# Layer 0 of a two-layer transformer backbone: background weight loads on GpSimd's queue, and attention A's value products two items later

## The chip, the cores and the metric

One Trainium2 chip, of which this program uses one core. The core has five engines that run their own instruction streams in order: TensorE (PE, matrix products), VectorE (DVE), ScalarE (ACT), GpSimd (POOL) and SyncE (SP, which here only issues DMA transfers). GpSimd can issue DMA transfers as well. The metric is device microseconds (us) for one execution of the whole program; the figure given for a kernel is the median of several runs.

## The reference

A diffusion backbone over 1024 latent tokens and 256 context tokens, width 1024, two layers. Layer 0, where the change lies, runs two attentions side by side and then a mixture of experts:

```
mod = silu(c) @ w_ada[l] + b_ada[l]              # modulation: 6 x 1024 numbers for x, the same for ctx
h   = x * (1 + sc1) + sh1
aq, ak, av, bq, bk, bv = split(h @ ab_w_in)
oa = window_gqa(rope(aq), rope(ak), av, ..., sink)   # A: 8 heads, 2 key heads, window 128 + context
ob = neighbourhood_attn(bq, bk, bv, ..., rpb)        # B: 8 heads, 8 x 16 neighbourhood + context
y  = concat(oa, ob) @ ab_w_out
x  = layer_norm(alpha * x + g1 * y);  then experts, and layer 1 in the same manner
```

Each attention is softmax(scores) times values. The modulation of both layers (`w_ada`, 2 x 1024 x 6144 numbers in float32) doesn't depend on the tokens, so most of it is computed in the background of layer 0's attention.

## The kernel before

Numbers are held as pairs of 16-bit floats (a high part and a rest), so that a product takes three matrix products (`mm3`, L183 to L185), and each probability block is split in two as well.

**Units.** `attn_l0` goes over six units u: two for A (four heads each) and four for B (two heads each). While unit u's attention runs (`attn_unit`), the projection of unit u+1 (`proj_unit`), 16 steps of the background modulation (`ada`, called `bg`) and a bias table are emitted between its steps (`interleave`, a hand-written mix by weights). A scheduler then sets the final order of each engine's instructions from this program order; the order of an engine is fixed before the run, and each engine works through its own in turn.

**One item** of attention is a pair (block t of 128 tokens, head h). It passes through the stages of `pipelined`: `qk` (scores S on PE, L679 to L682), `soft` (row maximum on DVE L702, L703, L705; exponential on ACT L706 for A, L720 and L723 for B; the high part `Ps` on ACT L730), `low` (the rest, on DVE or GpSimd, L737; after the odd head SP issues one DMA transpose for both heads, L739, which writes the transposed probabilities `PT`), two empty stages, and `pv` (value products O on PE from PT; after the last head DVE L771, ACT L774, GpSimd L775 and a store by GpSimd's queue, L776). In step i, `pv` therefore handles item i-5. `Ps` is a ring of two buffers (one per pair of heads), `PT` a ring of three, S has two buffers.

**The background modulation** works in steps n of 512 KB each: a load of `w_ada` (L311) into a ring of three buffers, the high part on ACT (L315), the rest on DVE (L318, which frees the buffer), products on PE (L331). Every fourth step ends a row (L337) that SP stores to DRAM (`mod_d`, L339); the row's start value, `b_ada`, is loaded by GpSimd's queue (L324). 16 of the 96 loads belong to an earlier stage, which passes `tps`; 80 are the background's.

Of the kernel before, what the change touches and what calls it, by code (L numbers as in the profile page):

```python
# [13 lines left out]
F16 = mybir.dt.float16  # L14
# [8 lines left out]
P = 128  # L23
# [50 lines left out]
def pipelined(items, stages):  # L74
    n, depth = len(items), len(stages)
    st = [None] * n
    for i in range(n + depth - 1):
        for s in (0, *range(depth - 1, 0, -1)):
            j = i - s
            if 0 <= j < n:  # L80
                st[j] = stages[s](items[j], st[j])
        yield
# [86 lines left out]
class Kern:  # L169
# [131 lines left out]
    def ada(self, work, pool, pspool, rbufs, hbufs, bbufs, tps=None):  # L301


        nc = self.nc
        raws, parts, rows, sums = {}, {}, {}, {}

        def load(n):
            l, j = work[n // 4]
            cols, k = slice(j * 512, (j + 1) * 512), n % 4 * 2
            raws[n] = pool.tile([P, 2, 512], F32, name="adaraw", bufs=rbufs)  # L310
            nc.sync.dma_start(raws[n], self.i["w_ada"][l].rearrange("(k p) n -> p k n", p=P)[:, k:k + 2, cols])  # L311

        def high(n):
            parts[n] = pool.tile([P, 2, 2, 512], F16, name="adahl", bufs=hbufs)
            nc.scalar.activation(parts[n][:, 0], raws[n], AF.Copy, scale=SW)  # L315

        def low(n):
            nc.vector.scalar_tensor_tensor(parts[n][:, 1], raws[n], SW, parts[n][:, 0], op0=ALU.mult, op1=ALU.subtract)  # L318

        def products(n):  # L320
            if n % 4 == 0:
                l, j = work[n // 4]
                rows[n // 4] = pool.tile([2, 512], F32, name="ada_b", bufs=bbufs)
                (nc.gpsimd if tps is None else nc.sync).dma_start(  # L324
                    rows[n // 4], self.i["b_ada"][l:l + 1, j * 512:(j + 1) * 512].to_broadcast([2, 512]))
                sums[n // 4] = pspool.tile([P, 512], F32, name="ps_ada", tag="proj")
            ps = sums[n // 4]
            for q in range(2):
                k = n % 4 * 2 + q
                for a in range(2):  # L330
                    nc.tensor.matmul(ps, self.sc(k), parts[n][:, a, q],  # L331
                                     start=k + a == 0, stop=k == KD - 1 and a == 1)

        def end(c):
            (l, j), row, ps = work[c], rows[c], sums[c]
            for part in (ps[:2], ps[32:34]):
                nc.vector.scalar_tensor_tensor(row, part, 1.0 / (SA * SW), row, op0=ALU.mult, op1=ALU.add)  # L337
            if j >= 4:
                nc.sync.dma_start(self.mod_d[l, :, j * 512:(j + 1) * 512], row)  # L339
                return  # L340
            pt = (tps or pspool).tile([P, 4, 2], F32, name="ps_adat", tag="O" if tps else "proj")
            for q in range(4):
                nc.tensor.transpose(pt[:, q, :], row[:, q * P:(q + 1) * P], self.id32[:2, :2])
            dst = self.modTs[l][:, j // 2, (j % 2) * 4:(j % 2) * 4 + 4, :]
            if j < 2:
                nc.vector.tensor_scalar_mul(dst, pt, SA)
            else:
                nc.vector.tensor_scalar(dst, pt, 1.0, SA, op0=ALU.add, op1=ALU.mult)

        last = 4 * len(work) - 1  # L350
        for n in range(-1, last + 1):
            for m in range(0 if n < 0 else n + rbufs - 1, min(last, n + rbufs - 1) + 1):
                load(m)
            if n < last:
                high(n + 1)
            if n >= 0:
                low(n)
                products(n)
                if n % 4 == 3:
                    end(n // 4)  # L360
                yield
# [83 lines left out]
def attn_l0(K, moe):  # L445
    nc, tc = K.nc, K.tc
    with ExitStack() as outer:
        big = K.pool("l0big", ctx=outer)
        ctx = outer.enter_context(ExitStack())
# [92 lines left out]
        vring = K.pool("l0v", 2, ctx=ctx)  # L542
        btab = K.pool("l0bt", 2, ctx=ctx)
        pring = K.pool("l0p", 2, ctx=ctx)
        tring = K.pool("l0t", 3, ctx=ctx)
        pctx = ctx.enter_context(ExitStack())
        rp = K.pool("l0rp", ctx=pctx, top=True)

# [83 lines left out]
        def attn_unit(u):  # L632
            isA = u < 2
# [13 lines left out]
            st_t = {}  # L647

            def blocks(t):
                if t >= NX:  # L650
                    return [], [8, 9]
                if isA:
                    return list(range(max(0, t - 1), min(NX, t + 2))), [8, 9]
                a, b = b_key_blocks(t)
                return list(range(a, b)), [8, 9]
# [30 lines left out]
            def soft(it, S):  # L686
                t, h = it
                loc, cx = blocks(t)
                nl, nk = len(loc) * P, (len(loc) + 2) * P
                if not isA and it == inner:  # L690
                    for r, n in ((0, 1), (8, 2)):
                        m = rowm[:, None, r:r + n, None].to_broadcast([P, 2, n, 64])
                        nc.gpsimd.tensor_add(tb[:, :, r + 3:r + 3 + n], tb[:, :, r + 3:r + 3 + n], m)
                if h == 0:
                    st_t[t] = (wk.tile([P, nh], F32, name="nm", tag=f"nm{nh}", bufs=3),
                               wk.tile([P, 2, nh], F32, name="dd", tag=f"dd{nh}", bufs=3))
                nm, dd = st_t[t]
                nmh = nm[:, h:h + 1]
                mx = wk.tile([P, 2], F32, name="mx", bufs=4)
                Pt = pring.tile([P, 896], F32, name="Pt")  # L700
                if isA:
                    nc.vector.reduce_max(mx[:, 0:1], S[:, :nk], axis=AX.X)  # L702
                    nc.vector.tensor_scalar(mx[:, 1:2], mx[:, 0:1], sinkb[:, gh0 + h:gh0 + h + 1], -ESC,  # L703
                                            op0=ALU.max, op1=ALU.mult)
                    nc.vector.tensor_scalar_add(nmh, mx[:, 1:2], LNSP)  # L705
                    nc.scalar.activation(Pt[:, :nk], S[:, :nk], AF.Exp, bias=nmh, scale=ESC,  # L706
                                         accum_out=dd[:, 0, h:h + 1])
                else:
                    nc.vector.reduce_max(mx[:, 0:1], S[:, nl:nk], axis=AX.X)
                    mm = mx[:, 0:1]  # L710
                    if nl:
                        mm = mx[:, 1:2]
                        i0 = loc[0] * 2 - 2 * t + 7
                        bt = tb[:, h, i0:i0 + nl // 64]
                        nc.vector.tensor_tensor_reduce(out=Pt[:, :nl], in0=S[:, :nl],
                                                       in1=bt.rearrange("p a b -> p (a b)"),
                                                       scale=1.0, scalar=mx[:, 0:1], op0=ALU.add, op1=ALU.max,
                                                       accum_out=mm)
                    nc.vector.tensor_scalar(nmh, mm, -ESC, LNSP, op0=ALU.mult, op1=ALU.add)
                    nc.scalar.activation(Pt[:, nl:nk], S[:, nl:nk], AF.Exp, bias=nmh, scale=ESC,  # L720
                                         accum_out=dd[:, 0, h:h + 1])
                    if nl:
                        nc.scalar.activation(Pt[:, :nl], Pt[:, :nl], AF.Exp, bias=nmh, scale=ESC,  # L723
                                             accum_out=dd[:, 1, h:h + 1])
                if h % 2 == 0:
                    st_t[t, "Ps"] = pring.tile([P, 4 * 896], F16, name="Ps")
                    st_t[t, h] = tring.tile([P, 28, P], F16, name="PT")
                Ps, PT = st_t[t, "Ps"], st_t[t, h - h % 2]
                a = (h % 2) * 2 * nk
                nc.scalar.activation(Ps[:, a:a + nk], Pt[:, :nk], AF.Copy)  # L730
                return Pt, Ps, PT, a, nk
# [48 lines left out]
            order = list(range(NT)) if isA else B_ORDER  # L780
            items = [(t, h) for t in order for h in range(nh)]
            inner = (2, 0)
            same = lambda i, s: s
            yield from pipelined(items, [qk, soft, low, same, same, pv])
            done.update(ended)
            if u == 5:
                for area in (qring, vring, btab, pring, tring):
# [1225 lines left out]
@with_exitstack  # L2013
def hybrid_backbone_kernel(ctx: ExitStack, tc: tile.TileContext, ins, out: bass.AP):
    nc = tc.nc
    K = Kern(ctx, tc, ins, out, None)
    K.setup()
    m0, m1 = Moe(K, 0, NT), Moe(K, 1, NX)
    attn_l0(K, m0)
    m0.run()  # L2020
    attn_l1(K, m1)
    final_ln(K, m1, lambda t: out[0, t * P:(t + 1) * P, :])
# [32 lines left out]
```

## Time and profile before

| | |
|---|---|
| Median of 3 runs (lowest, highest) | 3307.09 us (3301.38, 3307.56) |
| The profiled execution: its own time, its span | 3288.79 us, 3286.7 us |
| Busy over the span | PE 79%, DVE 79%, ACT 60%, GpSimd 31% |
| Attention A's units: scores from 105.8 us, last step's DVE work at 366.4 us | the stage 105 to 370 |
| Attention B's units | about 370 to 790 us |

A profile shows one execution: what each engine did and when, what ended its idle time (the releaser), and what the DMA queues moved. An engine's busy share is an average over the stage asked for. The rows below are word for word from such views.

### The profile page before, as it was taken

How to read it: one execution, taken by the hardware profiler on the slowest of the kernel's cores; microseconds unless marked ns; L12 is line 12 of the kernel's file. 1: busy time of each engine (PE TensorE's matmuls, PEld its weight loads, DVE VectorE, ACT ScalarE, POOL GpSimd, SP SyncE). 2: the span in 40 equal slices, each digit the busy share in tenths (PEclk: the TensorE clock that was granted, in tenths of full speed). 3: DMA queues.
4: the chain of work that ended last, by engine and by line, in shares of the span. 5: the costliest groups of instructions: out<-in, count | busy, mean ns of one | idle time of the engine just before them, and what ended most of it. 6: DMA issues, size and time to landing. Idle time of an engine off the chain costs nothing. (4 is left out here: it accounts for less than half of the span.)

```text
span 3286.7 us, 74447 instructions
## 1 busy us (share of the span) xinstructions
PE 2585.5 (79%) x30127; PEld 1790.8 (54%) x30127; DVE 2600.0 (79%) x4496; ACT 1974.0 (60%) x2949; POOL 1018.0 (31%) x652
## 2 busy tenths in 40 slices
PE   6877878868479888987477777877868489998886
PEld 3555545534267777765245554555534367776663
DVE  6787777778897777887767776778877897888986
ACT  5567766754466566776356655556653565666664
POOL 0133333332342222221532322222321473234443
PEclk8999999979789999998679988999978699999998
DMA  7789989789778889998538999645558598999996
GB/s 247 161 179 193 199 202 190 170 208 222 249 264 335 314 328 360 366 377 336 195 102 160 172 159 178 126 99 99 113 125 213 184 345 329 353 376 379 385 373 250
DMA packets 879160, 790.05 MB, mean 240 GB/s; under 512 B 689398, under 2 KB 719366, under 8 KB 878806
## 3 DMA queue, kind: packets, MB, share of 16 engines
q1 hardware_dynamic: 846981, 714.26, 75.4%
q0 software_dynamic: 26336, 69.85, 6.5%
q8 instruction: 239, 3.92, 0.5%
q10 hardware_dynamic: 5488, 1.09, 0.2%
q14 instruction: 116, 0.94, 0.1%
HBM read 565.85 MB, written 64.55 MB: 192 GB/s over the span
## 5 line engine op out<-in xcount | busy, mean ns | idle before, releaser
L375 DVE SCALAR_TENSOR_TENSOR arena<-arena 128x2048 f16<-128x2048 f32 (+4 forms) x439 | 911.1, 2098 | 174.4 <-ACT arena L374 170.3
L374 ACT ACTIVATE arena<-arena 128x2048 f16<-128x2048 f32 (+4 forms) x439 | 748.6, 1725 | 307.5 <-DMA arena<-in_w_gate_up_dram 197.3
L1364 PE MATMUL pg<-arena 128*128 128x72 f16 (+4 forms) x4736 | 635.2, 210 | 93.0 <-DVE arena L1351 70.6
L1366 PE MATMUL pg<-arena 128*128 128x72 f16 (+4 forms) x4736 | 631.9, 210 | 31.1 <-DVE arena L375 22.3
L1365 PE MATMUL pg<-arena 128*128 128x72 f16 (+4 forms) x4736 | 632.5, 210 | 10.0 <-DVE arena L1351 7.5
L183 PEld LDWEIGHTS <-arena 128*128 128x128 f16 (+1 forms) x3488 | 346.7, 103 | 356.0 <-DMA arena<-arena 148.5
L1365 PEld LDWEIGHTS <-arena 128*128 128x128 f16 x4736 | 473.9, 102 | 70.2 <-issue 66.3
L1366 PEld LDWEIGHTS <-arena 128*128 128x128 f16 x4736 | 473.3, 102 | 56.6 <-DVE arena L375 33.3
L1364 PEld LDWEIGHTS <-arena 128*128 128x128 f16 x4736 | 473.9, 102 | 32.9 <-ACT arena L374 18.8
L184 PEld LDWEIGHTS <-arena 128*128 128x128 f16 (+1 forms) x3488 | 346.5, 103 | 194.0 <-issue 99.4
L1381 POOL DMA_INDIRECT y_d<-arena,rt_sidx x74 | 237.9, 3215 | 606.3 <-ACT arena L1394 305.6
L185 PEld LDWEIGHTS <-arena 128*128 128x128 f16 (+1 forms) x3488 | 346.8, 103 | 128.5 <-issue 20.6
L183 PE MATMUL O<-arena 128*128 128x64 f16 (+1 forms) x1744 | 233.5, 210 | 142.7 <-DMA arena<-arena 108.9
L184 PE MATMUL O<-arena 128*128 128x64 f16 (+1 forms) x1744 | 233.0, 210 | 0.0
L185 PE MATMUL O<-arena 128*128 128x64 f16 (+1 forms) x1744 | 232.9, 210 | 0.0
L1774 POOL TENSOR_TENSOR arena<-arena 128x1280 f16<-128x1280 f32 x57 | 151.6, 2659 | 248.6 <-issue 166.0
L1755 ACT ACTIVATE arena<-S,arena 128x1280 f32<-128x1280 f32 x128 | 169.1, 1321 | 92.7 <-DVE arena L1753 81.0
L1344 POOL DMA_INDIRECT arena<-h_d,rt_gidx x74 | 147.3, 1990 | 223.8 <-PE pt L1350 162.4
L1752 DVE TENSOR_REDUCE arena<-S 128x1 f32<-128x1280 f32 x128 | 189.6, 1482 | 26.5 <-PE S L185 17.6
L195 PE MATMUL py<-arena 128*72 128x512 f16 (+4 forms) x592 | 185.9, 395 | 20.7 <-ACT arena L1376 13.9
L197 PE MATMUL py<-arena 128*72 128x512 f16 (+4 forms) x592 | 183.5, 392 | 0.0
L199 PE MATMUL py<-arena 128*72 128x512 f16 (+4 forms) x592 | 180.4, 386 | 0.0
(390 smaller groups left out, 6261.7 us busy)
## 6 DMA issues: line engine op xcount, KB each, us to landing
arena<-in_w_gate_up_dram SPq DMA_DIRECT2D x256, 1024.0 KB
arena<-in_w_down_dram SPq DMA_DIRECT2D x128, 1024.0 KB
arena<-in_w_ada_dram SPq DMA_DIRECT2D x96, 512.0 KB
arena<-y_d SPq DMA_DIRECT2D x36, 512.0 KB
x_d<-arena POOLq DMA_DIRECT2D x18, 512.0 KB, 3.5
h_d<-arena SPq DMA_DIRECT2D x18, 512.0 KB
arena<-x_d SPq DMA_DIRECT2D x18, 512.0 KB
arena<-in_x_dram SPq DMA_DIRECT2D x16, 512.0 KB
```

The source lines that it names most:

```text
L183: mm(ps, lh, rh, start=first, stop=False)
L184: mm(ps, lh, rl, start=False, stop=False)
L185: mm(ps, ll, rh, start=False, stop=last)
L195: mm(ps[:, o], lh, rh[:, o], start=first, stop=False)
L197: mm(ps[:, o], lh, rl[:, o], start=False, stop=False)
L374: nc.scalar.activation(wh, raw, AF.Copy, scale=scale)
L375: nc.vector.scalar_tensor_tensor(wl, raw, scale, wh, op0=ALU.mult, op1=ALU.subtract)
L1364: mm(pg[:, m, :n], wh, xh, start=k == 0 and m % 4 == 0, stop=False)
L1365: mm(pg[:, m, :n], wh, xl, start=False, stop=False)
L1366: mm(pg[:, m, :n], wl, xh, start=False, stop=k == 7 and m % 4 == 3)
L1381: self.K.nc.gpsimd.indirect_dma_start(out=self.K.y_d[self.l], out_offset=bass.IndirectOffsetOnAxis(ap=sidx, axis=0), in_=y[:n], in_offset= ...
L1752: nc.vector.reduce_max(mx[:, 0:1], S[:, :TOK], axis=AX.X)
```

## The change

Three edits, all in layer 0's attention. The background's loads of `w_ada` and the stores of its rows go out on GpSimd's queue and no longer on SP's. In A, two further empty stages stand between `low` and `pv`, so `pv` handles item i-7 in step i; B keeps two. The transposed probabilities get one area of 84 blocks in place of a ring of three tiles of 28 blocks (the same bytes): A cuts it into four slots of 20 blocks, B into three of 28, and the slot follows from the pair's place in its unit, starting at slot 0 in each unit.

```
-            nc.sync.dma_start(raws[n], self.i["w_ada"][l]...)
+            (nc.gpsimd if tps is None else nc.sync).dma_start(raws[n], self.i["w_ada"][l]...)
...
             if j >= 4:
-                nc.sync.dma_start(self.mod_d[l, :, j * 512:(j + 1) * 512], row)
+                nc.gpsimd.dma_start(self.mod_d[l, :, j * 512:(j + 1) * 512], row)
...
-        tring = K.pool("l0t", 3, ctx=ctx)
+        tring = K.pool("l0t", 1, ctx=ctx)
+
+        PTs = tring.tile([P, 84, P], F16, name="PT")
...
-                    st_t[t, h] = tring.tile([P, 28, P], F16, name="PT")
+                    n = items.index(it) // 2 % (4 if isA else 3)
+                    st_t[t, h] = PTs[:, 20 * n:20 * n + 20] if isA else PTs[:, 28 * n:28 * n + 28]
...
-            same = lambda i, s: s
-            yield from pipelined(items, [qk, soft, low, same, same, pv])
+            same = [lambda i, s: s] * (4 if isA else 2)
+            yield from pipelined(items, [qk, soft, low, *same, pv])
```

The edits add two lines in front of the attention's functions and one more in `soft`, so L702, L737, L739, L771, L775 and L776 of before are L704, L740, L742, L774, L778 and L779 after.

Two places show what this does to the order of instructions. The first is DVE's stream where the first block of the first A unit ends; L771 (L774 after) takes that block's value products O, L702 (L704) a row maximum of a later item, L737 (L740) the rest of a probability block. Before:

```order
L621 COPY arena<-arena 128x64
L771 TENSOR_TENSOR arena<-O,arena 128x256
L337 SCALAR_TENSOR_TENSOR arena<-ps_ada,arena 2x512
L625 SCALAR_TENSOR_TENSOR arena<-ps_proj,arena 128x64
L703 TENSOR_SCALAR arena<-arena 128x1
L737 TENSOR_TENSOR arena<-arena 128x640
L705 TENSOR_SCALAR arena<-arena 128x1
L702 TENSOR_REDUCE arena<-S 128x1
```

After:

```order
L623 COPY arena<-arena 128x64
L705 TENSOR_SCALAR arena<-arena 128x1
L627 SCALAR_TENSOR_TENSOR arena<-ps_proj,arena 128x64
L337 SCALAR_TENSOR_TENSOR arena<-ps_ada,arena 2x512
L740 TENSOR_TENSOR arena<-arena 128x640
L707 TENSOR_SCALAR arena<-arena 128x1
L704 TENSOR_REDUCE arena<-S 128x1
L774 TENSOR_TENSOR arena<-O,arena 128x256
```

The block's end stands one item further back: one more row maximum and one more rest go ahead of it. Counted over PE's whole order of A (80 items): where the value products of item j begin, PE has begun the scores of 5.4 items from j on before the change, on average, and of 6.3 after it; over B's 80 items it is 5.5 and 5.4.

The second place is GpSimd's stream where the first B unit ends and the second begins. L737 (L740) with 128x256 is the rest of a context block of the new unit, L775 (L778) and L776 (L779) end a block of the old one. Before:

```order
L737 TENSOR_TENSOR arena<-arena 128x896
L775 TENSOR_TENSOR arena<-arena 128x128
L776 DMA o_d<-arena 256x1x128
L737 TENSOR_TENSOR arena<-arena 128x256
L775 TENSOR_TENSOR arena<-arena 128x128
L776 DMA o_d<-arena 256x1x128
```

After:

```order
L740 TENSOR_TENSOR arena<-arena 128x896
L778 TENSOR_TENSOR arena<-arena 128x128
L779 DMA o_d<-arena 256x1x128
L311 DMA arena<-in_w_ada_dram 128x2x512 x3
L778 TENSOR_TENSOR arena<-arena 128x128
L339 DMA mod_d<-arena 2x512
L779 DMA o_d<-arena 256x1x128
L740 TENSOR_TENSOR arena<-arena 128x256
```

Three loads and a store now stand in GpSimd's stream, and the rest of the context block stands behind them and behind the end of the old unit's last block.

## Rows read from the trace of the kernel before

**Rows 1.** The stages A and part of B: busy us and instructions of each engine.

```profile
core 0: us, PE busy (x) PEld busy (x) DVE busy (x) ACT busy (x) POOL busy (x), PEclk, DMA share, GB/s
105.00:370.00 265.00, 209.01 (x2274) 138.54 (x2273) 215.30 (x567) 178.23 (x398) 80.73 (x88) 0.95 0.90 188
370.00:700.00 330.00, 258.00 (x2611) 157.71 (x2610) 249.09 (x586) 229.16 (x507) 113.34 (x114) 0.92 0.88 196
```

**Rows 2.** PE's waits, 105 to 370 us: total, times, longest.

```profile
PE O L183 <- DMA arena<-arena: 40.1, 27, 3.4
PE S L679 <- ACT arena L706: 12.8, 13, 2.5
```

**Rows 3.** DVE's waits, 105 to 370 us.

```profile
DVE arena L702 <- PE S L682: 19.9, 18, 3.4
DVE arena L771 <- PE O L185: 5.8, 6, 2.0
...
DVE arena L702 <- PE S L680: 3.4, 4, 1.9
```

**Rows 4.** ACT's waits, 105 to 370 us.

```profile
ACT arena L730 <- DMA arena<-arena: 10.6, 10, 2.5
```

**Rows 5.** The timeline of A, 196 to 219 us, by engine: start, duration, wait and releaser.

```profile
197.62 0.23 PE L183 MATMUL O<-arena 128*128 128x64 f16 x1 [3.27 <-DMA arena<-arena]
211.94 0.20 PE L183 MATMUL O<-arena 128*128 128x64 f16 x1 [2.11 <-DMA arena<-arena]
...
199.50 0.42 DVE L771 TENSOR_TENSOR arena<-O,arena 128x256 f32<-128x256 f32 x1 [2.00 <-PE O L185]
212.64 0.69 DVE L737 TENSOR_TENSOR arena<-arena 128x512 f16<-128x512 f32 x1 [1.76 <-ACT arena L730]
...
211.98 0.63 ACT L730 ACTIVATE arena<-arena 128x512 f16<-128x512 f32 x1 [1.77 <-DMA arena<-arena]
```

**Rows 6.** The loads L311 (ns, first and last start) and who waits for them (us, times).

```profile
L311 SPq DMA_DIRECT2D arena<-in_w_ada_dram x96: 367/453/1450, 1.3 to 640.0; - x96
...
  ACT arena L315: 2.9, 2
```

**Rows 7.** SP's queue, 105 to 700 us: what the loads waited for.

```profile
SPq L311 <- DVE arena L318: 22.7, 15, 3.4
```

**Rows 8.** DMAs that GpSimd issues: its time for one (min/median/max ns), and for an indirect one.

```profile
L776 POOL DMA_DIRECT2D o_d<-arena x60: 675/680/751, 134.7 to 795.7; - x60
DMA to landing us min/median/max: 2.0/4.1/7.2
...
L1381 POOL DMA_INDIRECT y_d<-arena,rt_sidx x74 | 237.9, 3215 | 606.3 <-ACT arena L1394 305.6 <-DVE arena L1392 204.5 <-ACT arena L1373 42.6
```

**Rows 9.** A load and the ACT work on its data, 241 to 249 us.

```profile
241.91 0.37 SPq L311 DMA_DIRECT2D arena<-in_w_ada_dram  x1
...
247.93 1.06 ACT L315 ACTIVATE arena<-arena 128x1024 f16<-128x1024 f32 x1
```

**Rows 10.** GpSimd in B, 385 to 615 us, and SP and PE behind it.

```profile
389.16 1.65 POOL L737 TENSOR_TENSOR arena<-arena 128x768 f16<-128x768 f32 x1 [5.81 <-ACT arena L730]
...
475.19 0.66 POOL L737 TENSOR_TENSOR arena<-arena 128x256 f16<-128x256 f32 x1 [5.77 <-ACT arena L730]
481.22 1.26 POOL L775 TENSOR_TENSOR arena<-arena 128x128 f16<-128x128 f32 x1 [5.37 <-ACT arena L774]
...
610.85 1.74 POOL L737 TENSOR_TENSOR arena<-arena 128x768 f16<-128x768 f32 x1
...
478.86 1.64 SPq L739 DMA_TRANSPOSE arena<-arena  x1
...
490.97 0.19 PE L183 MATMUL O<-arena 128*128 128x64 f16 x1
496.91 0.19 PE L183 MATMUL O<-arena 128*128 128x64 f16 x1
```

**Rows 11.** PE's waits, 370 to 700 us.

```profile
PE O L183 <- DMA arena<-arena: 19.0, 10, 3.9
```

More of the change, by code (lines that the diff above doesn't have):

```diff
@@ L310, in load @@
             raws[n] = pool.tile([P, 2, 512], F32, name="adaraw", bufs=rbufs)
-            nc.sync.dma_start(raws[n], self.i["w_ada"][l].rearrange("(k p) n -> p k n", p=P)[:, k:k + 2, cols])
+            (nc.gpsimd if tps is None else nc.sync).dma_start(raws[n], self.i["w_ada"][l].rearrange("(k p) n -> p k n", p=P)[:, k:k + 2, cols])
         def high(n):
```

## The prediction

> **What bounds the kernel now.** I asked first for the busy times of layer 0's attention by stage [rows 1]. In A's 265 us no engine is full: DVE is busy 215.3 us (81%), PE 209.0 (79%), ACT 178.2, GpSimd 80.7. So waits in order, not throughput, make up the stage, and the next view is who waits for whom. PE's largest wait in A is that of the value products for the transposed probabilities: 40.1 us in 27 waits, none over 3.4 us; the next is 12.8 us for a free score buffer [rows 2]. PE's waits matter because DVE, the busiest engine, in turn waits for PE: 19.9 + 3.4 us for scores and 5.8 us for finished products, 29.1 us of its 49.7 us idle [rows 3]. In the timeline the reader sees this passed on: PE stands 3.27 us until a transpose has landed, and DVE's L771 behind it stands 2.00 us [rows 5].
>
> The same landing has a second waiter. ACT's L730 writes the `Ps` buffer that the transpose two pairs earlier reads; at 211.9 us PE, ACT and DVE all stand for one landing (2.11, 1.77 and 1.76 us) [rows 5]. Over A this second wait costs ACT 10.6 us in 10 waits [rows 4].
>
> In B, PE waits 19.0 us in 10 waits for transposes out of 330 us [rows 11]; nothing in the edit's stages changes there.
>
> **The change part by part.**
>
> *Value products later (A).* The edit says two items, the order says less: 5.4 becomes 6.3. An item of A takes 265 / 80 = 3.3 us, so a transpose gets about 0.9 x 3.3 = 3.0 us more before PE wants it. The mean wait is 40.1 / 27 = 1.5 us and the longest 3.4, so nearly all of the 40.1 us goes from PE. What that is worth to the stage is read from DVE: it can gain at most the 29.1 us in which it stood for PE. Of PE's two waits together (52.9 us) the transposes make 76%, so 29.1 x 0.76 = 22 us of it come from them. The second waiter stays, for `Ps` still has two buffers: matching each L739 of A with the L730 two pairs later (36 pairs inside the units), the trace has L730 start within 0.4 us of the landing in 11. In those 11 of 36 ACT is at the door with PE, and what PE saves ACT keeps. That leaves 22 x 25/36 = 15 us. Bounds: 0, if every pair goes that way, and 29 us, if DVE loses all its waits for PE. I take 15, since 25 of 36 pairs have room. The last items of a unit are not held up more: the order puts the next unit's scores ahead of them before and after.
>
> *The loads on GpSimd.* SP loses 80 issues of 0.45 us and their waits for a free buffer (22.7 us for L318 alone) [rows 6, 7]. Little stood behind them: setting each L739 against the end of its rest L737, it starts 0.33 us late on average in A and 0.62 in B, and in only five of 80 cases is it a load or store of the modulation that holds it over 1 us. I put this at 1 us.
>
> GpSimd gains 80 loads and 16 stores. The trace has no 512 KB load on that queue; the nearest row is L776 at 0.68 us (675 to 751 ns over 60), the dearest issue of GpSimd is the indirect scatter at 3.2 us [rows 8]. I take 0.68, the same kind of plain transfer, and keep 3.2 as the upper bound. Busy time is no matter (54 us in 595, beside 194 busy). What counts is the stream's order. I took the new order of GpSimd, gave each old instruction its time in the trace and each load its buffer's release (the L318 three steps back). The loads would then go out 0.7 us earlier than from SP on average: GpSimd is mostly at the door before the buffer is free. ACT needs the data late: of load and L315 matched in turn, the median lead is 17 us and the shortest in the row shown is 6.0 [rows 9]; a plain transfer of GpSimd lands in 4.1 us (2.0 to 7.2) [rows 8], and on ACT the loads cost 2.9 us in two waits today [rows 6]. One load, at the border of A and B, gets behind the end of the last block and would come 6 us late; that is in the margin below.
>
> Behind the loads stands L737 on GpSimd. It would start late in B seven times, 31 us in all (first at 389.16, last at 610.85) [rows 10], and 12 us in A. The worst is the border shown with the change: the context rest that ran at 475.19 now stands behind L775, which ended at 481.22 + 1.26, a store and a second issue, so it starts 8.5 us later and with it the transpose of 478.86. Its products began only at 496.9 us, so 8.5 us hurt nobody there; that is the cover. Where there is none, at 10 of the 33 transposes of this stretch of B (PE's waits) [rows 11], the lateness reaches PE: 31 x 10/33 = 9 us, of which by A's ratio of stage gain to PE's wait (22/40) 5 us arrive. Bounds: 0, all of it covered, and the full 9 us. The 12 us in A fall into the 3.0 us that each transpose has gained.
>
> At 3.2 us an issue, the same reckoning makes L737 late by 92 us in B and 63 us in A: 92 x 10/33 = 28 us on PE in B, and A's 63 us (22 cases, 2.8 us each) use up the new room.
>
> The Trainium skill speaks against the move here: "SBUF — State Buffer", section "SBUF: two separate sides", says that GpSimd writes the descriptors of its own transfers itself and is locked out while VectorE runs an instruction that takes both of the ports they share. The trace disagrees as far as it goes: L776 took at most 751 ns in 60 issues beside a DVE busy 75 to 81% [rows 1, 8]. By the rule the issue would stretch towards the upper bound and the sum would be that of the slower rival below; by the rows it is 0.68.
>
> *One area for PT.* The bytes are the same. A keeps a distance of four pairs, B of three, but each B unit starts again at slot 0, where the unit before left its tenth pair: the first transpose of a unit waits for the last pair's products. At the second such border that moves 572.97 to 575.9 us and at the first 472.35 to 477; the pair's own products came at 491 us [rows 10], so it costs nothing there, and about 1 us at the third, where they follow at once.
>
> *Sum.* -15 (A) - 1 (SP) + 5 (GpSimd in B) = -11 us, the border's 1 us and the one late load being within the rounding. On the profiled execution (span 3286.7, its own time 3288.8) that is 3277.8. The median of the runs shown is 18 us above that execution, so I subtract from the median: 3307 - 11 = **3296 us**.
>
> **The rivals.**
>
> *The wait changes its owner (same).* Every pair goes the way of those at 143, 158, 184, 198, 212 and 224 us: with PE no longer standing, DVE and ACT come earlier to the next L730 and stand there for the same landing. For it: 10 of the 18 odd pairs start L730 within 0.1 us of the landing, and a round of two pairs (a transpose of 5.5 us, then 6 to 9 us of DVE and ACT work up to the next) is as long as the 13.2 us that two pairs take. Against: even pairs have 0.7 to 6.7 us of room, and DVE's 2.00 us behind L771 lies inside such a round and does go. It gives 0 - 1 + 5: 3311 us, within the bound.
>
> *GpSimd's queue becomes the path (slower).* If a load holds GpSimd for about 2 us or more, L737 comes late in 13 or more cases in B, and A's room is used up. At 3.2 us: 28 us more on PE in B at the full rate, A's gain halved to 8: 3307 - 8 + 28 = 3327 us; it decides from about 2 us an issue. Against it stand L776's rows.
>
> *All of it (faster).* DVE loses its 29.1 us, B is covered: 3307 - 29 - 1 = 3277 us.
>
> **How the numbers follow.** Timing this kernel can tell a difference of about 0.2% (6.6 us) from none. Forecast (gain of 7 to 20 us) 0.40; all of it (over 20) 0.15; the wait changes its owner 0.27; GpSimd's queue 0.18. So faster 0.55, same 0.27, slower 0.18. The range goes from 3279, near the full gain, to 3314, past the unchanged case and into the slower one's lower part; the forecast's own range is 3287 to 3300.
>
> **What the profile after would show.** If right: PE's wait for transposes in A falls from 40.1 us to under 12, ACT's for them rises from 10.6 to some 15 to 20, DVE's for scores falls, and A's stage (first scores to last block's end) shortens by about 15 us; GpSimd's L311 takes some 0.7 us; ACT's wait for `w_ada` stays under 10 us; PE's wait for transposes in B stays within 19 +- 8. Wrong, if ACT's wait takes up what PE loses, if L311 on GpSimd takes over 2 us, or if PE's wait in B doubles.

## The result, and the profile after

The changed kernel takes 3335.8 us (median of 4 runs, 3331.2 to 3342.0) against 3306.9 us: 29 us slower, a ratio of 1.010 (95% interval 1.0083 to 1.0117). I had forecast 3296 us. The profiled execution has a span of 3334.1 us.

First by stage, as in [rows 1], on the changed kernel (stretch, its length, then busy us and instructions of PE, PEld, DVE, ACT, GpSimd; granted clock; DMA share; GB/s):

```profile
105.00:370.00 265.00, 202.30 (x2125) 134.66 (x2123) 200.55 (x517) 162.89 (x357) 99.05 (x113) 0.92 0.82 171
370.00:700.00 330.00, 267.56 (x2571) 161.91 (x2570) 220.07 (x563) 217.69 (x490) 145.09 (x161) 0.92 0.90 176
```

The same 265 us hold fewer instructions on every engine but GpSimd (DVE 517 against 567), so A's stage got longer. To see how much, I set the starts of the first, 40th and 80th transpose of the probabilities side by side; the kernel before stands twice, since I had it profiled again (below):

```
us between transposes:   1st to 40th (A)   40th to 80th (B)   80th to the end
before                        250.6              414.1            2505.2
before, second profile        258.0              413.5            2516.3
after                         271.9              437.1            2503.7
```

The loss lies in attention: 14 to 21 us in A, 23 in B, and 3 to 5 before the first transpose (121.4 us, against 116.8 and 118.3); what follows has no part in it. PE's granted clock in A is 0.92, where it was 0.95 (0.93 in the second profile), a mean over stretches at 2.4 and 1.2 GHz. By these rows one matmul keeps PE busy for 95 ns on average where it was 92, or some 7 us over the 2274 of A (an estimate); whether a part of the loss came that way no run separates. Next, who waits for whom in A (105 to 370 us: total, times, longest), the lines that answer to [rows 2 to 4]:

```profile
PE O L183 <- DMA arena<-arena: 37.2, 17, 5.8
ACT arena L733 <- DMA arena<-arena: 31.1, 13, 6.7
DVE arena L704 <- PE S L684: 27.6, 17, 7.2
...
DVE arena L704 <- PE S L682: 2.9, 2, 2.8
...
DVE arena L774 <- PE O L185: 0.6, 1, 0.6
```

PE waits for transposes fewer times (17, not 27), but longer (up to 5.8 us, not 3.4). ACT's wait for them trebled, 10.6 to 31.1 us. In B (370 to 700 us) PE's wait rose from 19.0 [rows 11] to

```profile
PE O L183 <- DMA arena<-arena: 43.6, 14, 5.5
```

The loads themselves look harmless (the line's view on the changed kernel: issue time in ns min/median/max, first and last start; who waits for the data; issue to landing):

```profile
L311 POOL DMA_DIRECT2D arena<-in_w_ada_dram x80: 709/732/930, 43.5 to 687.1; - x80
...
  ACT arena L315: 4.5, 1
...
DMA to landing us min/median/max: 4.1/5.2/11.4
```

So an issue takes 0.73 us as I had supposed, and its data come in time. What has become late is the transposes. I measured each from the end of ACT's L730 (L733) of the odd head to its issue by SP, and from the issue to the last of its 16 landing events in the trace. The first part hardly moved: 1.77 to 1.73 us on average in A, 2.80 to 2.81 in B. GpSimd, with 96 more issues, holds up the rests no more than before. The second part, the flight, grew from 5.14 to 6.30 us in A and from 6.23 to 7.68 in B (one flight over 16 us left out).

One pair shows it. SP's and ACT's timeline of the kernel before, tenth pair (start, duration, wait and releaser; "x2" stands for two instructions run together):

```profile
174.81 0.53 SPq L311 DMA_DIRECT2D arena<-in_w_ada_dram  x1
177.36 7.41 SPq L739 DMA_TRANSPOSE arena<-arena  x2
...
185.95 0.39 SPq L311 DMA_DIRECT2D arena<-in_w_ada_dram  x1
...
184.01 0.74 ACT L730 ACTIVATE arena<-arena 128x640 f16<-128x640 f32 x1 [2.52 <-DMA arena<-arena]
```

and the same pair in the changed kernel, SP, GpSimd and ACT:

```profile
179.68 10.11 SPq L742 DMA_TRANSPOSE arena<-arena  x2
...
177.50 0.72 POOL L311 DMA_DIRECT2D arena<-in_w_ada_dram  x1 [5.17 <-DVE arena L707]
...
180.57 0.69 POOL L779 DMA_DIRECT2D o_d<-arena  x1 [0.30 <-POOL arena L778]
183.13 0.72 POOL L311 DMA_DIRECT2D arena<-in_w_ada_dram  x1 [1.87 <-DVE arena L318]
...
189.87 0.74 ACT L733 ACTIVATE arena<-arena 128x640 f16<-128x640 f32 x1 [4.45 <-DMA arena<-arena]
```

Before, SP is busy issuing two transposes for 7.41 us, and a load can only go out after them, into the same queue; the first transpose landed 6.6 us after its issue. After, GpSimd issues a load 3.5 us into the transpose's flight, and the transpose takes 10.1 us. ACT stands 4.45 us for its landing instead of 2.52. The pair is not a clean one: a store of O by GpSimd (L779, 128 KB) also went out 0.9 us into that flight, where in the kernel before the like store (L776) had gone out 2.1 us ahead of the transpose.

### The profile page after: what moved, and what is told of

Read it like the earlier page. It is cut to its first block, busy times and chain, and to the rows that moved or that the text cites. A ratio compares the mean times of both kernels' runs of the same rounds, so it can differ in the third digit from the quotient of the medians.

```text
span 3334.1 us, 74425 instructions
## 1 busy us (share of the span) xinstructions
PE 2610.3 (78%) x30127; PEld 1803.5 (54%) x30127; DVE 2602.3 (78%) x4496; ACT 1972.9 (59%) x2949; POOL 1085.1 (33%) x748
## 5 line engine op out<-in xcount | busy, mean ns | idle before, releaser
L1368 PE MATMUL pg<-arena 128*128 128x72 f16 (+4 forms) x4736 | 639.1, 211 | 10.1 <-DVE arena L1354 6.7
L183 PE MATMUL O<-arena 128*128 128x64 f16 (+1 forms) x1744 | 230.5, 209 | 166.5 <-DMA arena<-arena 136.9
L185 PE MATMUL O<-arena 128*128 128x64 f16 (+1 forms) x1744 | 230.2, 209 | 0.0
L184 PE MATMUL O<-arena 128*128 128x64 f16 (+1 forms) x1744 | 230.0, 209 | 0.0
```

The lines of the kernel that those rows point to most:

```text
L183: mm(ps, lh, rh, start=first, stop=False)
L184: mm(ps, lh, rl, start=False, stop=False)
L185: mm(ps, ll, rh, start=False, stop=last)
L1368: mm(pg[:, m, :n], wh, xl, start=False, stop=False)
```

## The experiments

Two theories went into the first runs. **Q:** GpSimd's order loses the time; it stands for DVE's results with rests behind it. **D:** the load's bytes run on a second queue beside a transpose in flight, where on SP's queue they ran behind it or ahead of it. A third, **L**, was that the later products lose by themselves. Medians of the kernel before in the three groups of runs were 3305.1, 3301.9 and 3300.7 us.

**The later products and the PT area alone.** Loads and stores stay on SP.

```
 nc.sync.dma_start(raws[n], ...)                       # as before
 nc.sync.dma_start(self.mod_d[l, ...], row)            # as before
+same = [lambda i, s: s] * (4 if isA else 2)           # and the PT area, as in the change
```

> The later value products and the one area for PT alone; loads and stores of the modulation on SP as before. Theory Q (GpSimd's queue is what lost the time: its loads and stores wait for DVE and hold the rests behind them, so transposes are issued late): the loss is gone, 3290 to 3307 us, and PE's wait for transposes in A falls well below 40 us. Theory L (the later products lose by themselves: the block's end further back, scores and rests of later items ahead of it): most of the 29 us stays, 3325 to 3340 us. My prediction's first step says 3292 us.

3282.8 us, ratio 0.9941 (0.9918 to 0.9964): 20 us faster. L falls; this part of the change does what I said of it, and the loss is the other part's. The waits in A (same columns):

```profile
PE O L183 <- DMA arena<-arena: 21.5, 15, 3.4
ACT arena L733 <- DMA arena<-arena: 19.0, 13, 3.6
DVE arena L704 <- PE S L684: 9.5, 14, 1.6
...
DVE arena L774 <- PE O L185: 2.3, 2, 1.4
DVE arena L704 <- PE S L682: 1.0, 3, 0.5
```

DVE's waits for PE go from 29.1 us [rows 3] to 12.8, and part of PE's wait is now ACT's.

**The queues alone.**

```
+(nc.gpsimd if tps is None else nc.sync).dma_start(raws[n], ...)
+nc.gpsimd.dma_start(self.mod_d[l, ...], row)
```

> Loads and stores on GpSimd's queue alone; products and PT as before. Theory Q: 3325 to 3350 us, PE's wait for transposes in A above 40 us, GpSimd standing for L318 and L337 with rests behind it. Theory D (the loads are no longer in one queue with the transposes but run beside them, and each transpose takes longer in flight): the same time, but with the transposes issued about as early as before and landing a microsecond or more later after their issue. Theory L: 3300 to 3312 us.

3363.0 us, ratio 1.0182 (1.0157 to 1.0208): 58 us slower, more than any theory had. Waits in A:

```profile
POOL arena L311 <- DVE arena L318: 64.4, 10, 44.0
...
PE O L183 <- DMA arena<-arena: 56.5, 20, 6.2
ACT arena L730 <- DMA arena<-arena: 23.5, 10, 4.6
```

PE and ACT stand 80 us for transposes, where it was 51 [rows 2, 4]. GpSimd does stand for its buffers (44.0 us of the first row before the stage's first load), but that holds no transpose up: from L730 to the issue it takes 1.77 us on average, as before, and the flight has a mean of 6.11 us. That is D's sign, not Q's.

**The area alone.** `PTs` with three slots of 28 for A and B, products two stages behind.

> One area for PT alone, cut into three slots of 28 blocks for A and B, each unit starting at slot 0; products two stages behind as before. Theories Q, L and D: 3303 to 3311 us, no change that can be measured. If the restart at slot 0 or one tile for all slots costs something by itself (a transpose that waits for readers of another slot): 3315 us or more.

3292.9 us, ratio 0.9970 (0.9953 to 0.9987): 10 to 12 us faster, which no theory had. Its stages (A 254.0, B 415.2 us) are within those of the two profiles of before, so where the gain comes from stays open. It does say that of the 20 us above about half belong to the later products and half to the area. PE's wait for transposes in A is as long as before, so its fall above belongs to the later products:

```profile
PE O L183 <- DMA arena<-arena: 40.0, 27, 3.6
```

**The loads alone on GpSimd**, stores on SP.

> Only the 80 loads on GpSimd's queue; the 16 stores of the modulation's rows stay on SP. Theory Q splits here: if it is the stores that stand in GpSimd's queue for DVE's row (L337), this kernel is 10 us or more below the one with loads and stores; if it is the loads, it is within 6 us of that one. Theory L: 3300 to 3312 us.

3387.7 us, ratio 1.025 (1.0225 to 1.0276): 83 us slower, so the loads are the cost, and the stores on GpSimd give 25 us of it back; I had expected at least 10 us less than with loads and stores there, or the same. Where the 25 us come from stays open. The transposes go out a little later here in A (2.04 us after L730) and not in B (2.79); SP stands up to 10.0 us at once for a row's store, but in B, and at most 1.0 us in A. GpSimd's L324, which needs the row's buffer free again, stands 54.4 us in all for the store's landing (105 to 800 us), against 32.7 with the stores on its own queue.

The trace of these kernels lets D be looked at transpose by transpose. I sorted A's 40 by the loads about them: none in flight; one issued before and not landed ("ahead"); one issued after it and at least 1.5 us before its landing ("behind"); both. Count and mean flight in us:

```
                       none       ahead      behind      both      all
before               10: 4.29   16: 5.80    8: 4.62    6: 5.50    5.14
before, 2nd profile  10: 4.27   16: 5.88    9: 4.85    5: 5.60    5.21
products and area     9: 4.23   12: 5.61    7: 5.78   12: 6.04    5.46
after                11: 4.29   15: 6.30    3: 7.48   11: 7.98    6.30
queues alone          9: 3.99   15: 5.97    6: 6.81   10: 7.79    6.10
loads alone           9: 4.04   17: 6.19    7: 6.78    7: 7.66    6.07
loads on ACT         12: 4.36   12: 5.23   10: 7.06    6: 8.05    5.85
```

With no load near, a transpose flies 4.0 to 4.4 us in each of these. With a load ahead it flies 0.9 to 2.2 us longer on whichever queue. With a load behind it flies 0.3 to 1.6 us longer where both go through SP's queue, and 2.7 to 3.2 where the load has a queue of its own.

The last figure isn't the load's alone. Many of these flights also had a store of O by GpSimd issued in them (in the four kernels with a queue of its own, between 4 and 8 of the 14 to 16 in "behind" and "both"), and a longer flight has more time for a load to fall into it. So I also asked only for loads and stores issued within 2.5 us of a transpose's issue, took A's 32 large transposes in each of the ten profiles with whole loads (the seven of the table, the area alone, and two of the runs below: the change without its loads and the third buffer), and compared each transpose with those at the same place in the order (least squares). A load on a queue of its own then costs 2.2 us (+-0.5, 26 cases) and a store 1.0 (+-0.4); on SP's queue almost no load goes out that early (6 cases).

**The same issues, a sixteenth of the bytes.** GpSimd issues and waits as in the change; SP moves the rest.

```
+nc.sync.dma_start(raws[n][:, :, 32:], src[:, :, 32:])
+nc.gpsimd.dma_start(raws[n][:, :, :32], src[:, :, :32])
```

> The kernel before, with each of the 80 loads split: SP loads 480 of every 512 columns, GpSimd the other 32, so GpSimd has the same 80 issues and the same waits for a free buffer, but 1/16 of the bytes beside the transposes. Theory D (what costs is that the load's bytes run on a second queue beside a transpose in flight): 3300 to 3320 us, and a transpose of A with a load issued behind it takes about 4.6 us as in the kernel before. Theory Q (what costs is GpSimd standing in its order): 3360 to 3390 us, like loads alone on GpSimd.

3307.2 us, ratio 1.0014 (1.0000 to 1.0028). The time decides for D against Q. GpSimd stands for its buffers about as long as with whole loads (56.5 and 64.4 us in A; 107.1 and 107.9 over A and B), and the rests stand behind it as there, at a price of 0 to 9 us. PE and ACT together stand for transposes as long as before (51 us in A):

```profile
POOL arena L316 <- DVE arena L323: 56.5, 11, 42.4
...
PE O L183 <- DMA arena<-arena: 33.9, 23, 3.1
...
ACT arena L735 <- DMA arena<-arena: 17.4, 13, 2.1
```

D's other sign did not come. The mean flight in A is 5.37 us, close to the 5.14 and 5.21 of before, but the six transposes with a load behind alone took 6.71 us and not 4.6; three of them had a store of O issued in their flight, and the other three took 5.50. Six are too few to say more.

What is nearly gone is the second stream of bytes. The queues in A (packets, MB, share of 16 engines' time; q1 holds what SP issues, q0 what GpSimd issues), in the kernel before,

```profile
q1 hardware_dynamic: 121369, 46.97, 86.1%
q0 software_dynamic: 1168, 2.53, 3.2%
```

in this one,

```profile
q1 hardware_dynamic: 118554, 44.42, 82.4%
q0 software_dynamic: 2113, 3.44, 5.5%
```

and in the changed kernel:

```profile
q1 hardware_dynamic: 103953, 27.62, 56.6%
q0 software_dynamic: 5392, 17.36, 24.5%
```

**Half of the bytes**: 256 of 512 columns on GpSimd.

> As with 32 columns on GpSimd, but 256 of every 512: half of each load's bytes run on GpSimd's queue beside the transposes, the issues and waits of GpSimd are the same. Theory D (bytes beside a transpose in flight): between the two ends measured, 3307 us with 1/16 of the bytes there and 3388 us with all of them, so about 3335 to 3355 us, mean flight of A's transposes 5.5 to 6.0 us. Theory Q in the form that only a real load's issue holds GpSimd: near 3307 or near 3388 us, not between.

3318.6 us, ratio 1.0061 (1.0038 to 1.0084): 18 us slower. It lies between the ends and the mean flight in A, 5.61 us, is as D expected, but the time is lower than I wrote. In order of bytes on the second queue (1/16, 1/2, all) the loss is 5, 18 and 83 us: more bytes cost more, but the first half costs far less than the second. A flight half a microsecond longer is partly absorbed by slack that a whole one uses up; that is a reading of mine, no run separates it.

**Another second queue.** ACT issues the loads, GpSimd nothing more.

> The kernel before with the 80 loads issued by ACT: a queue other than SP's again, and GpSimd has nothing more to do. Theory D: transposes of A with a load issued during their flight take 6.5 us or more (4.6 before, 6.8 with the loads on GpSimd), their mean in A rises by about 1 us, and the time by 30 us or more. Theory Q: transposes as before (mean 5.1 us in A); the time moves only by what ACT's own waits for a free buffer cost. If the long flights belong to GpSimd's queue alone, flights stay near 4.6 us too, and the time says which part is ACT's.

3365.9 us, ratio 1.0189 (1.0166 to 1.0213). Flights with a load behind take 7.06 us, so long flights do not belong to GpSimd's queue alone. Nor does the size of the packets explain them: in the traces the loads move in packets of 4096 bytes from GpSimd, but of 2048 from ACT, as from SP. The 64 us are not all theirs: the mean flight rose by only 0.7 us in A and 0.3 in B, where the stage is still 28 us longer, and transposes also go out 0.6 us later after L730 in A. How much is ACT standing for buffers I can't tell apart.

**The change without its loads**: later products, area, stores on GpSimd.

> The change without its loads: the later products, one area for PT, and the 16 stores of the modulation's rows on GpSimd; loads on SP. With loads on GpSimd the stores there were worth 24 us (3363 against 3388). If that came from SP's transposes no longer standing behind a store that waits for its row, it is to be had here too: 3265 to 3280 us. If it came only from the two queues together: 3278 to 3290 us, as without the stores.

3284.5 us, ratio 0.9945 (0.9925 to 0.9965), the same as without the stores. Their 25 us exist only beside loads on GpSimd.

**A third buffer for Ps**, with the later products, loads and stores on SP.

```
+PPs = tring.tile([P, 17920], F16, name="PT")    # A: 3 slots for Ps, 4 for PT; B: 2 and 3
```

> The later products with a third buffer for Ps in A (the same bytes in all: Ps and PT share one area, A cuts it into 3 and 4 slots of 20 blocks, B into 2 and 3 of 28); loads and stores on SP. My prediction's second waiter (ACT's L730 stands for the transpose two pairs earlier, 19.0 us in A with the later products) would go: ACT's wait for transposes in A under 5 us, 5 to 12 us faster than with two buffers (3283), 3270 to 3278 us. If that wait only moves on to the next engine: 3278 to 3290 us.

3284.7 us, ratio 0.9943 (0.9922 to 0.9964): no more than with two buffers. In A ACT's L735 no longer waits for any transpose, but the waits move on (A, same columns):

```profile
PE O L183 <- DMA arena<-arena: 31.0, 20, 3.8
PE S L681 <- ACT arena L708: 16.7, 17, 4.0
ACT arena L315 <- PE ps_ada L331: 16.1, 7, 4.8
```

PE's wait for transposes rises again from 21.5 to 31.0 us, and ACT, now further ahead, waits 16.1 us for the background's products. A's stage is 241.1 us against 245.2, B's 418.1 against 415.0.

**The kernel before once more.**

> The kernel before, profiled once more, to see how far two profiles of one kernel differ by stage: stage A from first to last transpose 250.6 us and B 414.1 us in the profile that I predicted from, all theories expect both within 6 us of that, and the part after the last transpose within 15 us of 2505 us.

3308.2 us. A took 258.0 us here, 7 more than in the profile that I predicted from and past the 6 that I had allowed, B 413.5, the rest 2516.3: a single profile's stage A is good to some 7 us, and the part after attention to some 11.

## Why the prediction was wrong, by its own steps

*Value products later: the right sign and the right mechanism, a smaller size.* I took -15 us. Products and area together gave -20 (-27 to -12), the products alone about half; that the two come near 15 is in part luck. The mechanism was the one described, at half strength: PE's wait in A fell to 21.5 us (I had said under 12), ACT's rose to 19.0 (I had said 15 to 20), and DVE won 16.3 of its 29.1 us. My count of L730 at the landing was one short (12 of 36, and 11 of the 18 odd pairs, start there), which would make the term 14.7. The second waiter is real, but not the limit that I took it for: without it the kernel gains nothing more. In the full change this gain shows as the difference to the queues alone, 3363 to 3336 us: 27 us, so the parts don't quite add (-20 and +58 would be +38, where 29 was measured).

*The loads on GpSimd: the step that failed.* The terms -1 (SP) and +5 (GpSimd in B) have measured +58 us (ratio 1.0182) together. Everything that I priced in this step came out: the issue takes 0.73 us, the data come in time (ACT waits 4.5 us for them, I had said under 10), and what GpSimd's order costs is 0 to 9 us by the run with a sixteenth of the bytes, where I had 5. What I left out is the transfer itself. I asked when a load is issued and who stands behind the issue, and took a load's bytes to cost the same on any queue. The rows to ask were there: the DMA engines are busy 90% of A [rows 1], and 86.1 of these 90 points go to the one queue of SP, in which the transposes that PE and ACT wait for and the loads stand in one order. On SP's queue of the kernel before, a load issued after a transpose hardly slowed it (4.62 against 4.29 us); on its own queue it slows it by about 2 us, with GpSimd's stores set apart. As I read these figures, the one queue had been giving the urgent transfer precedence over the patient one, whose data are wanted 17 us later; the change took that away. How a flight about 1 us longer on average turns into 58 us is not worked out.

The Trainium skill has the pieces of this. "DMA: Bandwidth & Descriptors", section "Issuing engines are not separate DMA queues", says that transfers issued by different engines run on the same 16 DMA engines and interleave, and that a second issuing engine saves only issue time; the equal flights without a load and the longer ones with one agree. The same page of the Trainium skill, section "Queues, rings and completion order", says that each DMA engine alternates between the queues that have work, packet by packet. By that rule a load issued behind a transpose moves up beside it on a second queue, which the column "behind" agrees with; the alternation itself no view here shows.

*GpSimd's order in B.* I had L737 31 us late there. Measured from L730 to the transposes' issue, nothing is later on average (2.80 and 2.81 us).

*The rivals.* "GpSimd's queue becomes the path" (0.18) had the right sign and the wrong mechanism: it needed an issue of 2 us or more, the longest was 0.93. The rule of the Trainium skill that I weighed against the move ("SBUF — State Buffer", section "SBUF: two separate sides") left no mark: beside a DVE busy 76% of A (200.6 of 265 us) the 80 issues stayed between 0.71 and 0.93 us. Whether DVE ran the kind of instruction that the rule speaks of, no view here shows. "The wait changes its owner" described ACT's 31.1 us, but as a consequence of longer flights, not as a loss of the gain. Of the signs that I had named for being wrong, PE's wait in B did double (19.0 to 43.6 us), and ACT's wait in A rose by 20.5 us while PE's fell by 2.9; the issue of L311 stayed under 2 us.

*One area for PT.* I had it at nothing. It gives some 10 us by the run with the area alone, from a place that the profiles don't show.

## What to carry over

Ask of a transfer that is moved to another queue not only who waits behind its issue, but which urgent transfer it ran behind on the old queue: sharing a queue is an order, and a second queue gives it up. Where the DMA engines are near full, as here (90% of A), try first to keep transfers with slack on the same queue as those that an engine stands for, issued after them. And test the parts of a change apart: here two parts together were worth 20 us and the third cost 58, and the version without the third (3283 us) beats both kernels.

## What the runs showed of the hardware

A transpose of A's probabilities flies 3.9 to 4.7 us on average when no load of `w_ada` is near, over all kernels run here, and 6.8 to 8.1 us when a 512 KB load is issued from another engine during its flight, whether that is GpSimd or ACT; by the comparison above about 2 us of this are the load's own, and the rest goes with stores issued in the same flights and with loads ahead. An issue of such a load took 0.73 us on GpSimd and 0.37 on ACT (medians). The loss isn't proportional to the bytes on the second queue: 5, 18 and 83 us for 1/16, 1/2 and all.
